# State loads asked for later, token sums moved to DVE, and four later slices in a one-core decoder step

## The chip, the core and the metric

The kernel runs on one core of a Trainium2 chip. A core has TensorE (PE, matmuls), VectorE (DVE), ScalarE (ACT), GpSimd (POOL) and SyncE (SP), which here issues the loads. The metric is the device time of one execution in microseconds; lower is better. Times are medians of runs; the profile is of one execution.

## The reference

One step of a hybrid decoder layer: 512 prompt tokens and 8 x 4 sample tokens (544 columns in all) go through one input projection of width 2048 to 8192, eight heads of stick-breaking attention and eight heads of the HGRN2 recurrence, a gated per-head norm and an output projection. All in 32-bit floats.

```
h = rmsnorm(x, norm_w);  p = h @ w_in            # q_a k_a v_a z_a | q_b f_b i_b z_b
o_a = stick_breaking(q_a, k_a, v_a)              # prompt: causal blocks; samples: 16 cached pages each
...
S_new = S * exp(bl) + (kc * exp(bl - b)).T @ vc  # per head, state 128 x 128; samples start from state_s
o_b = (qc * exp(b)) @ S + tril(qc @ kc * decay) @ vc
...
x = x + concat(norm(o_a) * silu(z_a), norm(o_b) * silu(z_b)) @ w_out;  y = rmsnorm(x, final_norm_w)
```

Outputs are the two results, the new keys and values, and the new states of the prompt and of the eight samples.

## The kernel before

Every large product is made of fp32r parts: an operand is split into a rounded half (ACT, `L304`) and a remainder (DVE, `L305`), and three products are added. A projection of 128 columns (`project`) has 24 slices of STEP = 4 units of matmuls; its two accumulators are emptied by DVE (`L454`, `L456`), and the next projection needs the same two banks.

The program runs in five stages. First the tokens are transposed and split. Then four query heads are projected plainly (`first_part`, up to 107 us), and beside them `token_sums` makes four sums of token blocks in hi and lo halves. With these, eleven pairs of column blocks are projected by a scheme of Strassen's kind with seven products for eight (`project_two`, to 340 us); their results go to DRAM. In the attention stage (to 785 us) keys and values of head h are projected, and beside them runs `attend` for the head before. In the HGRN2 stage (to 1317 us) the forget gate and input of head h are projected, and beside them `hgrn` of the head before: four score rounds (first the pairs, `finish_pairs`, then the three of ROUNDS), the update of the states (`up`, `usp`) and the outputs. The output projection ends the program.

Beside both stages runs `decode`, the attention of the samples to their cached pages, in 36 steps: a step loads two units of key pages (SP, `L687`, three buffers), DVE transposes them (`L697`), PE multiplies them (`dzp`, `L825`), and four steps later the values (`av`, `L835`) use pages from ten buffers (`L708`).

The order on PE and SP is the order in which the program is written (a manual schedule), and that is set by `Flow`: the projection's slices are the base, and after each slice up to two side slices are taken whose wait is over. A side generator yields (cost, wait, hold of a bank, share of the base that must be done); the wait is in a modelled time that adds up slice costs. So a number such as 4000.0 at `finish_head` says how many modelled nanoseconds must pass before the slice is put into PE's order. It sets the order alone: in the run every instruction waits for its operands, and what stands behind it on its engine waits too. DVE, ACT and POOL are ordered by the program's scheduler.

`finish_head` squares a head's output (POOL `L565`, `L569`; ACT `L568`), sums the squares on PE (`sp`, `L572`, `L573`) and stores the head. `hgrn` asks at its start for the head's sample states (`L875`, two tiles `bst`, two buffers in all); they are used at `osp` (`L1023`) and updated at `usp` (`L1052`, `L1055`) and stored from there by POOL (`L1057`). So the request of head h waits on SP until both stores of head h-1 are done.

Of the kernel before, what the change touches and what calls it, by code (L numbers as in the profile page):

```python
# [18 lines left out]
P = 128  # L19
# [11 lines left out]
H = 8  # L31
# [111 lines left out]
def hybrid_step(ctx: ExitStack, tc: tile.TileContext, x_prompt, x_sample, cache_k, cache_v, state_s, page_table,  # L143
# [316 lines left out]

    def token_sums(c):

# [9 lines left out]
        def less(eng, a, b):  # L472
            d, e = temp(), temp()
            eng.tensor_tensor(d, a[0], b[0], ALU.subtract)
            eng.tensor_tensor(e, a[1], b[1], ALU.subtract)
            eng.tensor_tensor(d, d, e, ALU.add)
            return d
# [11 lines left out]

        t1 = less(nc.vector, block(0, 1), block(0, 0))  # L490
        keep_sum(nc.vector, 0, t1)
        t2 = less_sum(nc.vector, block(1, 1), t1)
        keep_sum(nc.vector, 1, t2)
        keep_sum(nc.gpsimd, 3, less_sum(nc.gpsimd, block(1, 0), t2))
        keep_sum(nc.gpsimd, 2, less(nc.gpsimd, block(1, 1), block(0, 1)))

# [105 lines left out]
    def attend(h, qt, kt, vt):  # L602
# [56 lines left out]
        a_past[h] = True  # L659
        yield from finish_head(ap, h, ot, zt, 4000.0)  # L660

# [130 lines left out]
    def decode(start, stop):  # L792
# [4 lines left out]
        for step in range(NSTEP):  # L797
# [14 lines left out]
            while values and weights_ready[b - 1] is None:  # L812
                yield 0.0, 500.0, 0.0, 0.0
            yield (32 * 56.0 if keys else 0.0) + (8 * 213.0 if values else 0.0), \
                (8000.0 if step == 0 else 3000.0), 0.0, start + (stop - start) * step / NSTEP
            if keys:
# [38 lines left out]
    def hgrn(h, F, it, res):  # L855
# [15 lines left out]
        nc.gpsimd.tensor_tensor(prod[0], f2[:, :, 0], f2[:, :, 1], ALU.mult)  # L871
        sts = []
        for hf in range(2):
            st = bp_.tile([P, 4, P], F32, name="bst", bufs=2)
            nc.sync.dma_start(st, state_s[0, 4 * hf:4 * hf + 4, h].rearrange("b k v -> k b v"))  # L875
            sts.append(st)

# [37 lines left out]

        yield from scores(1, lambda n: e0[:, n * 192:(n + 1) * 192], e0[:, 688:816], 5000.0, finish_pairs)
        e = etile()
# [7 lines left out]
        for r, hl in enumerate(ROUNDS):  # L925
# [20 lines left out]
            def finish(half, sp):  # L946
# [10 lines left out]
                if half and r == 0:  # L957
# [4 lines left out]
                    nc.vector.copy_predicated(a5, m5, s5)  # L962

            yield from scores(hl, moving, e[:, 824:952] if r == 0 else None, 3000.0, finish)
            new = etile()
# [78 lines left out]
        if finish:  # L1044
            yield from finish_head(bp_, H + h, ot, res["zt"], 4000.0)
        for hf in range(2):
# [40 lines left out]

    SUMS_AT = ((1, 4), (1, 18), (2, 8), (2, 22))
    sp_ = None
    sstack = ExitStack()  # L1090

    def first_part():
        nonlocal sp_
        for h in range(PLAIN):
# [6 lines left out]
            for i, c in enumerate(project(qtile, h * P, h == 0)):  # L1101
# [6 lines left out]
                if (h, i) in SUMS_AT:  # L1108
                    token_sums(SUMS_AT.index((h, i)))
                yield c  # L1110
# [324 lines left out]
```

## Time and profile before

| | us |
|---|---|
| runs of the kernel | 1557.32 and 1562.46, median 1559.89 |
| the profiled execution | 1562.26 |
| its span, first to last instruction | 1560.5 |
| PE busy (matmuls) | 1359.2 (87%) |
| DVE / POOL / ACT busy | 879.1 / 507.6 / 473.4 |
| mean granted clock of PE | 0.933 |

The difference of 1.8 us between the execution's time and its span lies around the first and last instruction. A row of the wait view gives the waiting engine and line, what released it, and the time. PE works its slices strictly in order, so a wait of PE delays all that follows; an idle engine that nobody waits for costs nothing.

### The profile page before, as it was taken

To read this page: it belongs to the slowest core of one execution; us is meant where nothing else is said; L and a number is where in the kernel's file an instruction comes from. 1 tells how busy PE (TensorE), PEld (TensorE's weight loads), DVE (VectorE), ACT (ScalarE), POOL (GpSimd) and SP (SyncE) were. 2 spreads that over 40 slices of the span, in tenths; PEclk is the share of its full clock that TensorE was granted. 3 is DMA by queue.
4 is the path that set the end of the run, shared out by engine and by line. 5 is a ranking of instruction groups with operands and counts; after the bars stand their busy time and mean duration, and the time that the engine had idled before them with its cause. 6 is when DMAs were issued, how large, how long until landed. Compare 5 with 4: busy or idle time off the path is not lost.

```text
span 1560.5 us, 30699 instructions
## 1 busy us (share of the span) xinstructions
PE 1359.2 (87%) x11658; PEld 1215.6 (78%) x11658; DVE 879.1 (56%) x1427; ACT 473.4 (30%) x783; POOL 507.6 (33%) x723
## 2 busy tenths in 40 slices
PE   7769999998878979879878768989989889999997
PEld 6659999997766868768767557777868657889897
DVE  6866666645465554564665455576574745622223
ACT  6223343331333333333323031222222222422223
POOL 3777776650222221121222131232231222310101
PEclk9979999998988989999979879999989989999999
DMA  6224434439767967878844929898959656442223
GB/s 186 82 82 137 124 111 123 138 113 228 199 166 193 267 184 226 243 191 253 227 130 127 226 95 263 237 254 222 254 144 280 171 180 222 151 140 82 76 76 140
DMA packets 248965, 270.85 MB, mean 174 GB/s; under 512 B 14073, under 2 KB 170290, under 8 KB 248114
## 3 DMA queue, kind: packets, MB, share of 16 engines
q1 hardware_dynamic: 240048, 239.88, 55.8%
q0 software_dynamic: 6992, 21.08, 3.8%
q10 hardware_dynamic: 1778, 7.93, 1.4%
q8 instruction: 92, 1.51, 0.4%
q14 instruction: 55, 0.45, 0.1%
HBM read 244.16 MB, written 24.67 MB: 172 GB/s over the span
## 4 chain that ended last, share of the span: by engine, by line
PE 39%; issue 9%; DVE 8%; DMA 8%; ACT 3%; POOL 2%; SPq 1%; DVEq 0%; POOLq 0%; ACTq 0%
PE pacc L447 15%; PE yacc L1272 10%; PE av L835 4%; DVE kpage L697 3%; DMA kpage<-in_cache_k 3%; PE dzp L825 3%; PE sp L897 2%; DMA wraw<-in_w_in 1%; PE ysp L1281 1%; DMA ys<-in_x_sample 1%; PE usp L1052 1%; DVE wlo L305 1%; DMA m_dram<-sq 1%; PE op L655 1%; POOL sqlo L569 1%
## 5 line engine op out<-in xcount | busy, mean ns | idle before, releaser
L447 PE MATMUL pacc<-h_hi,whi 128*128 128x288 f32 (+1 forms) x1344 | 384.0, 314 | 40.2 <-DVE sq L456 25.3
L447 PE MATMUL pacc<-h_lo,whi 128*128 128x288 f32 (+1 forms) x1344 | 364.0, 298 | 0.0
L447 PEld LDWEIGHTS pacc<-h_hi,whi 128*128 128x128 f32 x1344 | 266.9, 199 | 71.7 <-issue 47.2
L447 PEld LDWEIGHTS pacc<-h_lo,whi 128*128 128x128 f32 x1344 | 267.4, 199 | 3.5 <-issue 1.7
L305 DVE TENSOR_TENSOR wlo<-wraw,whi 128x1024 fp32r<-128x1024 f32 x138 | 186.2, 1350 | 146.0 <-PE yacc L1272 70.3
L304 ACT CAST whi<-wraw 128x1024 fp32r<-128x1024 f32 x138 | 144.3, 1047 | 368.5 <-PE pacc L447 164.4
L447 PE MATMUL pacc<-h_hi,wlo 128*128 128x288 f32 (+1 forms) x1344 | 200.9, 297 | 0.0
L447 PEld LDWEIGHTS pacc<-h_hi,wlo 128*128 128x128 f32 x1344 | 181.1, 192 | 8.8 <-issue 8.0
L697 DVE STREAM_TRANSPOSE kpage<-kpage 128x2048 f32<-128x2048 f32 x64 | 146.3, 2298 | 20.2 <-DMA kpage<-in_cache_k 20.2
L825 PE MATMUL dzp<-kpage,qblk 128*32 128x128 f32 x2048 | 78.0, 306 | 67.5 <-DVE kpage L697 67.5
L1272 PE MATMUL yacc<-whi,m_hi 128*128 128x256 f32 x512 | 128.7, 290 | 0.0
L1272 PE MATMUL yacc<-whi,m_lo 128*128 128x256 f32 x512 | 124.9, 283 | 2.6 <-DVE m_lo L1262 2.6
L825 PEld LDWEIGHTS dzp<-kpage,qblk 128*32 128x32 f32 x2048 | 61.2, 123 | 79.7 <-DVE kpage L697 66.2
L1272 PEld LDWEIGHTS yacc<-whi,m_hi 128*128 128x128 f32 x512 | 97.4, 190 | 15.7 <-issue 12.4
L1272 PEld LDWEIGHTS yacc<-whi,m_lo 128*128 128x128 f32 x512 | 97.7, 191 | 3.2 <-DVE m_lo L1262 3.0
L835 PE MATMUL av<-vpage,dwt 128*32 128x512 f32 x512 | 88.1, 690 | 8.1 <-DMA vpage<-in_cache_v 8.1
L1344 POOL TENSOR_TENSOR y<-y,fnw 128x512 f32<-128x512 f32 (+1 forms) x18 | 25.2, 1419 | 179.8 <-DVE y L1340 110.5
L897 PE MATMUL sp<-bE,kr 128*128 128x192 f32 x256 | 52.0, 347 | 22.5 <-DVE kr L868 22.5
L305 DVE TENSOR_TENSOR wlo<-sraw,whi 128x1024 fp32r<-128x1024 f32 x33 | 52.4, 1589 | 28.5 <-ACT whi L304 28.5
L1272 PE MATMUL yacc<-wlo,m_hi 128*128 128x256 f32 x512 | 68.4, 282 | 0.1
L1272 PEld LDWEIGHTS yacc<-wlo,m_hi 128*128 128x128 f32 x512 | 64.3, 191 | 0.3 <-DVE wlo L305 0.3
L897 PEld LDWEIGHTS sp<-bE,kr 128*128 128x128 f32 x256 | 44.5, 203 | 24.6 <-issue 13.9
(344 smaller groups left out, 2522.7 us busy)
## 6 DMA issues: line engine op xcount, KB each, us to landing
kpage<-in_cache_k SPq DMA_DIRECT2D x256, 256.0 KB, 5.8
vpage<-in_cache_v SPq DMA_DIRECT2D x256, 256.0 KB, 5.2
wraw<-in_w_in SPq DMA_DIRECT2D x106, 512.0 KB, 6.0
wraw<-in_w_out SPq DMA_DIRECT2D x32, 512.0 KB, 3.4
sraw<-in_w_in SPq DMA_DIRECT2D x22, 512.0 KB, 5.4
p_dram<-so POOLq DMA_DIRECT2D x22, 272.0 KB, 2.9
bst<-in_state_s SPq DMA_DIRECT2D x16, 256.0 KB, 2.9
out<-bst POOLq DMA_DIRECT2D x16, 256.0 KB, 2.9
```

The costliest lines, as they stand in the source:

```text
L304: turns.append(nc.scalar.copy(hi, raw))
L305: nc.vector.tensor_tensor(lo, raw, hi.bitcast(F32), ALU.subtract)
L447: nc.tensor.matmul(ps[half][:, :n], a[:, j, :], x[:, j, ts], start=(kh == 0 and part == 0 and r == 0), stop=(kh == 1 and part == 1 and r = ...
L569: nc.gpsimd.tensor_tensor(lo, sq, hi.bitcast(F32), ALU.subtract)
L655: nc.tensor.matmul(op[:, tb * P:(tb + 1) * P], vn[:, j, :], wt[:, first[tb] + j, :], start=(j == 0), stop=(j == tb))
L697: nc.vector.transpose(flat, flat)
L825: nc.tensor.matmul(zp[32 * g:32 * g + 32, gp * P:(gp + 1) * P], qb[:, at:at + 32], kt[:, g, :, 32 * j:32 * j + 32], start=(gp == 0 and h2 ...
L835: nc.tensor.matmul(av[hf][32 * i:32 * i + 32, :], wt[:, gp, i, :], vpending[n], start=(gp == 0), stop=(gp == 3))
L897: nc.tensor.matmul(sp[:, i * 192:(i + 1) * 192], kr[:, n * P:(n + 1) * P], moving(n), start=True, stop=True)
L1052: nc.tensor.matmul(usp, kns, vb.rearrange("p b d -> p (b d)"), start=True, stop=True)
L1272: nc.tensor.matmul(out, m[4 * kq + j][:, c], b[:, j, :], start=(kq == 0 and part == 0 and r == 0 and (one or tb % 2 == 0)), stop=(kq == 3 ...
L1344: nc.gpsimd.tensor_tensor(part, part, fnw[:, cs].unsqueeze(1).to_broadcast([P, n, CG]), ALU.mult)
```

## The change

Three edits. `token_sums` is cut into two parts of four calls each, placed at eight points of the plain heads in place of four, with all its adds and subtracts on DVE; the third block sum no longer takes `t2` from the temporary but adds the halves of the second sum up again. Four waits of side slices become longer: `finish_head` of both kinds of heads 4000 to 6500, the key products of decode step 0 8000 to 18000, the first score round 5000 to 8000. The request for the sample states moves from the start of `hgrn` to the second round of ROUNDS, the third of the four score rounds.

```diff
--- before.py
+++ after.py
@@ -458,7 +458,7 @@
 
     sums = []
 
-    def token_sums(c):
+    def token_sums(part, c):
 
         j = slice(2 * c, 2 * c + 2)
         at = slice(0, XH), slice(XH, T)
@@ -487,12 +487,15 @@
             nc.scalar.copy(hi[:, j], x)
             eng.tensor_tensor(lo[:, j], x, hi[:, j].bitcast(F32), ALU.subtract)
 
-        t1 = less(nc.vector, block(0, 1), block(0, 0))
-        keep_sum(nc.vector, 0, t1)
-        t2 = less_sum(nc.vector, block(1, 1), t1)
-        keep_sum(nc.vector, 1, t2)
-        keep_sum(nc.gpsimd, 3, less_sum(nc.gpsimd, block(1, 0), t2))
-        keep_sum(nc.gpsimd, 2, less(nc.gpsimd, block(1, 1), block(0, 1)))
+        if part == 0:
+            t1 = less(nc.vector, block(0, 1), block(0, 0))
+            keep_sum(nc.vector, 0, t1)
+            keep_sum(nc.vector, 1, less_sum(nc.vector, block(1, 1), t1))
+        else:
+            keep_sum(nc.vector, 2, less(nc.vector, block(1, 1), block(0, 1)))
+            t2 = temp()
+            nc.vector.tensor_tensor(t2, sums[1][0][:, j].bitcast(F32), sums[1][1][:, j].bitcast(F32), ALU.add)
+            keep_sum(nc.vector, 3, less_sum(nc.vector, block(1, 0), t2))
 
     def project_two(pair, n, done):
         a = ps_acc.tile([P, 512], F32, name="pa", tag="acc")
@@ -657,7 +660,7 @@
         ot = ap.tile([P, SEQ], F32, name="ot", bufs=1)
         nc.vector.tensor_copy(ot, op)
         a_past[h] = True
-        yield from finish_head(ap, h, ot, zt, 4000.0)
+        yield from finish_head(ap, h, ot, zt, 6500.0)
 
 
     def page_value(held, b, gp, i):
@@ -812,7 +815,7 @@
             while values and weights_ready[b - 1] is None:
                 yield 0.0, 500.0, 0.0, 0.0
             yield (32 * 56.0 if keys else 0.0) + (8 * 213.0 if values else 0.0), \
-                (8000.0 if step == 0 else 3000.0), 0.0, start + (stop - start) * step / NSTEP
+                (18000.0 if step == 0 else 3000.0), 0.0, start + (stop - start) * step / NSTEP
             if keys:
                 if quarter == 0:
                     zp = ps_z.tile([P, 512], F32, name="dzp", tag="z")
@@ -869,11 +872,6 @@
         prod = [bp_.tile([P, n], F32, name=f"prod{n}") for n in (T // 2, 64, 16, 4)]
         tots = bp_.tile([P, DB], F32, name="tots")
         nc.gpsimd.tensor_tensor(prod[0], f2[:, :, 0], f2[:, :, 1], ALU.mult)
-        sts = []
-        for hf in range(2):
-            st = bp_.tile([P, 4, P], F32, name="bst", bufs=2)
-            nc.sync.dma_start(st, state_s[0, 4 * hf:4 * hf + 4, h].rearrange("b k v -> k b v"))
-            sts.append(st)
 
         yield 5 * TR, 900.0, 1500.0, 0.0
         tp = gbank("vtp")
@@ -913,7 +911,7 @@
                 nc.vector.tensor_tensor(a3, s3[:, :, 0:2], eye[:NS, :NS // 2], ALU.mult)
                 nc.vector.copy_predicated(a3[:, :, 1], sub[:NS, :NS // 2], s3[:, :, 2])
 
-        yield from scores(1, lambda n: e0[:, n * 192:(n + 1) * 192], e0[:, 688:816], 5000.0, finish_pairs)
+        yield from scores(1, lambda n: e0[:, n * 192:(n + 1) * 192], e0[:, 688:816], 8000.0, finish_pairs)
         e = etile()
         nat = e.rearrange("p (u y) -> p u y", y=14)[:, :, :8].rearrange("p u (j i) -> p u j i", i=2)
         ev = e3[:, :, 0:3:2].rearrange("p (u j) x -> p u j x", j=4)
@@ -961,6 +959,12 @@
                     s5 = sp[:NS, 456:].rearrange("p (u s i) -> p u s i", s=7, i=2)[:, :, 1:4:2]
                     nc.vector.copy_predicated(a5, m5, s5)
 
+            if r == 1:
+                sts = []
+                for hf in range(2):
+                    st = bp_.tile([P, 4, P], F32, name="bst", bufs=2)
+                    nc.sync.dma_start(st, state_s[0, 4 * hf:4 * hf + 4, h].rearrange("b k v -> k b v"))
+                    sts.append(st)
             yield from scores(hl, moving, e[:, 824:952] if r == 0 else None, 3000.0, finish)
             new = etile()
             grp = 4 if r < len(ROUNDS) - 1 else 1
@@ -1042,7 +1046,7 @@
         nc.vector.tensor_reduce(o_s[:, H + h, :], tp[:, :P].rearrange("p (j t) -> p t j", j=4), axis=AX.X, op=ALU.add)
         hg_past[h] = True
         if finish:
-            yield from finish_head(bp_, H + h, ot, res["zt"], 4000.0)
+            yield from finish_head(bp_, H + h, ot, res["zt"], 6500.0)
         for hf in range(2):
             vb = bp_.tile([P, NB, P], F32, name="bkn")[:NS]
             nc.gpsimd.tensor_tensor(vb, vs.unsqueeze(1).to_broadcast([NS, 4, P]),
@@ -1085,7 +1089,7 @@
         if col < W:
             nc.gpsimd.tensor_copy(q_new[:, col // P, :], out[:, SEQ:])
 
-    SUMS_AT = ((1, 4), (1, 18), (2, 8), (2, 22))
+    SUMS_AT = ((1, 2), (1, 10), (1, 18), (2, 2), (2, 10), (2, 18), (3, 4), (3, 12))
     sp_ = None
     sstack = ExitStack()
 
@@ -1106,7 +1110,7 @@
                     for n in range(4):
                         sums.append([sp_.tile([P, NK // 2, XH], F32R, name=f"sum{n}{m}") for m in ("hi", "lo")])
                 if (h, i) in SUMS_AT:
-                    token_sums(SUMS_AT.index((h, i)))
+                    token_sums(*divmod(SUMS_AT.index((h, i)), 4))
                 yield c
             store_part(h * P, qts[0])
         for n, pair in enumerate(couples):
```

The order on PE, counted in slices of the projections (four matmuls each) that stand ahead:

| slice | before | changed |
|---|---|---|
| key products of decode step 0, 1, 31 | 576, 610, 1403 | 598, 628, 1422 |
| last four value steps (32 to 35) | 1423, 1427, 1434, 1438 | 1442, 1446, 1446, 1446 |
| last slice ahead of the final gate's projection | 1446 | 1446 |
| sum of squares, attention heads 0 to 7 | 660, 706, 752, 798, 851, 895, 941, 990 | 662, 709, 758, 803, 849, 903, 947, 990 |
| first scores, HGRN2 heads 0, 1, 2 | 1000, 1051, 1092 | 1010, 1058, 1106 |
| sum of squares, HGRN2 heads 0, 1 | 1041, 1089 | 1050, 1104 |
| second state update of HGRN2 heads 0, 1 | 1055, 1096 | 1060, 1113 |

On DVE, in the third plain head's stretch; `so` are temporaries, `sum0lo` to `sum3lo` the low halves of the sums, `sq<-pacc` evictions, `wlo` a weight piece's remainder. Before:

```order
L305 TENSOR_TENSOR wlo<-wraw,whi 128x1024
L488 TENSOR_TENSOR sum1lo<-so,sum1hi 128x544
L474 TENSOR_TENSOR so<-h_hi_98 128x544
L475 TENSOR_TENSOR so<-h_lo_99 128x544
L476 TENSOR_TENSOR so<-so 128x544
L481 TENSOR_TENSOR so<-h_hi_100,so 128x544
L482 TENSOR_TENSOR so<-so,h_lo_101 128x544
L456 TENSOR_TENSOR sq<-pacc,rbc 128x256
```

In the changed kernel:

```order
L305 TENSOR_TENSOR wlo<-wraw,whi 128x1024
L488 TENSOR_TENSOR sum2lo<-so,sum2hi 128x544
L482 TENSOR_TENSOR so<-so,h_lo_101 128x544
L474 TENSOR_TENSOR so<-h_hi_100,h_hi_98 128x544
L475 TENSOR_TENSOR so<-h_lo_101,h_lo_99 128x544
L488 TENSOR_TENSOR sum3lo<-so,sum3hi 128x544
L476 TENSOR_TENSOR so<-so 128x544
L497 TENSOR_TENSOR so<-sum1hi,sum1lo 128x544
L456 TENSOR_TENSOR sq<-pacc,rbc 128x256
```

The third and fourth sums (`sum2lo`, `sum3lo`), which stood on POOL, now stand on DVE between the evictions, with the new add at `L497`.

On SP, around the state request of HGRN2 head 1 (`kr` a head's queries, `zt` its gate, `kpage` and `vpage` cached keys and values, `wraw` weights). Before:

```order
L708 DMA vpage<-in_cache_v 128x512
L559 DMA zt<-p_dram 128x544
L853 DMA kr<-p_dram 128x544
L257 DMA wraw<-in_w_in 128x8x128
L875 DMA bst<-in_state_s 128x4x128 x2
L257 DMA wraw<-in_w_in 128x8x128
L687 ISA
L687 DMA kpage<-in_cache_k 32x4x512
```

In the changed kernel:

```order
L711 DMA vpage<-in_cache_v 128x512
L966 DMA bst<-in_state_s 128x4x128 x2
L257 DMA wraw<-in_w_in 128x8x128 x2
L562 DMA zt<-p_dram 128x544
L856 DMA kr<-p_dram 128x544
L690 ISA
L690 DMA kpage<-in_cache_k 32x4x512
```

The request now stands behind the sixteen page loads of a decode step and ahead of two weight pieces, the head's own gate and head 2's queries; before, it stood right behind head 1's queries and a weight piece, ahead of a step's page loads.

## Rows read from the trace of the kernel before

**Rows 1.** Busy time by window, three stages: us and instructions, granted clock.
```profile
40.06:107.41 67.35, 40.72 (x291) 39.65 (x290) 49.35 (x46) 16.04 (x22) 54.46 (x36) 0.82 0.29 82
...
340.00:785.00 445.00, 372.48 (x3452) 331.47 (x3450) 247.38 (x371) 143.31 (x258) 99.84 (x201) 0.90 0.79 217
785.00:1317.50 532.50, 450.94 (x3944) 376.57 (x3943) 321.34 (x702) 122.89 (x192) 141.34 (x316) 0.91 0.73 203
```

**Rows 2.** Waits of PE, 40 to 108 us: total us, times, longest.
```profile
PE pacc L447 <- DVE sq L456: 25.3, 3, 16.8
```

**Rows 3.** The same view, PE, 340 to 785 us.
```profile
PE dzp L825 <- DVE kpage L697: 38.1, 9, 6.9
PE sp L573 <- POOL sqlo L569: 12.9, 5, 3.9
PE kvsp L176 <- DVE z L611: 4.9, 4, 3.5
...
PE vnp L176 <- DVE z L611: 2.8, 1, 2.8
```

**Rows 4.** The same view, PE, 785 to 1317.5 us.
```profile
PE dzp L825 <- DVE kpage L697: 29.5, 10, 9.3
PE sp L897 <- DVE kr L868: 22.5, 3, 10.6
PE sp L573 <- POOL sqlo L569: 9.0, 2, 7.3
PE av L835 <- DMA vpage<-in_cache_v: 8.1, 2, 7.5
```

**Rows 5.** The same view, SP's queue, 785 to 1317.5 us.
```profile
SPq L875 <- DMA out<-bst: 128.1, 12, 27.6
```

**Rows 6.** DVE by line, 40 to 108 us: busy us, mean ns, idle before.
```profile
L305 DVE TENSOR_TENSOR wlo<-wraw,whi 128x1024 fp32r<-128x1024 f32 x6 | 11.3, 1880 | 8.7 <-ACT whi L304 8.0 <-ACT sum1hi L487 0.7
...
L476 DVE TENSOR_TENSOR so<-so 128x544 f32<-128x544 f32 x4 | 4.9, 1230 | 0.1
...
L456 DVE TENSOR_TENSOR sq<-pacc,rbc 128x256 f32<-128x256 f32 x8 | 3.3, 415 | 0.1
L482 DVE TENSOR_TENSOR so<-so,h_lo 128x544 f32<-128x544 f32 x4 | 2.9, 722 | 0.1
L305 DVE TENSOR_TENSOR wlo<-ssum,whi 128x1024 fp32r<-128x1024 f32 x1 | 1.2, 1209 | 0.0
```

**Rows 7.** DVE by line, 43 to 46 us, where POOL stands.
```profile
L481 DVE TENSOR_TENSOR so<-h_hi,so 128x544 f32<-128x544 f32 x1 | 0.7, 725 | 0.0
```

**Rows 8.** Timeline, PE, decode step 0: start, us, idle before.
```profile
354.77 1.94 PE L825 MATMUL dzp<-kpage,qblk 128*32 128x128 f32 x32 [6.35 <-DVE kpage L697]
359.23 1.08 PE L825 MATMUL dzp<-kpage,qblk 128*32 128x128 f32 x16 [2.52 <-DVE kpage L697]
```

**Rows 9.** Busy time by window after a wait of PE; clock before DMA share.
```profile
92.00:95.00 3.00, 3.00 (x15) 3.00 (x15) 3.00 (x3) 0.00 (x0) 3.00 (x3) 0.50 0.00 0
96.00:99.00 3.00, 3.00 (x26) 3.00 (x25) 1.36 (x1) 0.65 (x1) 3.00 (x4) 1.00 0.06 15
```

**Rows 10.** Timeline, ACT, 364 to 366 us.
```profile
364.60 1.05 ACT L304 CAST whi<-wraw 128x1024 fp32r<-128x1024 f32 x1 [20.05 <-DMA wraw<-in_w_in]
```

**Rows 11.** Timeline, DVE, 378 to 385 us.
```profile
378.68 4.50 DVE L697 STREAM_TRANSPOSE kpage<-kpage 128x2048 f32<-128x2048 f32 x2
```

**Rows 12.** Timeline, SP, 852 to 864 us: HGRN2 head 1's states.
```profile
852.03 11.77 SPq L875 DMA_DIRECT2D bst<-in_state_s  x2
```

**Rows 13.** Timeline, PE, waits for key pages near 877 and 1165 us.
```profile
877.35 1.06 PE L825 MATMUL dzp<-kpage,qblk 128*32 128x128 f32 x13 [9.28 <-DVE kpage L697]
...
1164.96 1.30 PE L825 MATMUL dzp<-kpage,qblk 128*32 128x128 f32 x20 [3.35 <-DVE kpage L697]
```

**Rows 14.** The instructions of line 825: min/median/max ns, first and last start.
```profile
L825 PE MATMUL dzp<-kpage,qblk x2048: 272/273/424, 354.8 to 1245.2; 128*32 128x128 f32 x187
```

**Rows 15.** Timeline, SP, 1246 to 1254 us: eight value pages.
```profile
1247.00 6.20 SPq L708 DMA_DIRECT2D vpage<-in_cache_v  x8
```

## The prediction

> **What bounds the kernel now.** I read the busy times by stage first [rows 1]. From 40 to 107 us, the columns computed without Strassen's scheme, TensorE (PE) is busy 40.72 of 67.35 us, with DVE at 49.35 and POOL at 54.46. In the attention stage (340 to 785) PE is busy 372.48 of 445 us, in the HGRN2 stage (785 to 1317.5) 450.94 of 532.5. What can be won is PE's idle time: 27 us, then 73, then 82. The lists of who waited for whom name the causes. In the first stretch PE waits 25.3 us in three waits for the copies out of PSUM on DVE [rows 2]. In the attention stage the largest wait is for transposed key pages, 38.1 us in nine, then 12.9 us in five for the low half of the squares that POOL makes [rows 3]. In the HGRN2 stage it is key pages again (29.5 us in ten), then `kr` at a head's first score products (22.5 us in three, the longest 10.6), the squares (9.0) and value pages (8.1) [rows 4]. SP, the queue of all loads, stands 128.1 us in that stage at line 875, where a head asks for its sample states while their buffers are still being stored by the head before [rows 5].
>
> **Token sums.** PE's accumulators are emptied by DVE, which is slow while POOL works beside it: a weight piece's remainder takes 1880 ns on average and 1209 after POOL's share is done; of the sum ops, L476 takes 1230 ns, and L482, which mostly meets no POOL op, 722 [rows 6]. Between 43 and 46 us, with POOL idle, a sum op takes 725 ns [rows 7]. The change leaves POOL nothing of this and gives DVE 60 ops in place of 28 (the second sum is added up again from its halves, four ops more than the two engines had). In the changed order 57 of them stand before the eviction with which the Strassen part may start, with six weight remainders and nine evictions. At the lengths without POOL: 57 x 0.72 = 41.0, 6 x 1.21 = 7.3, and 9 evictions of at most 0.415 are 3.7, together 52.0 us from 40.06: the Strassen part starts at 92.1, now at 107.41: **-15.3**. DVE stays the bound there; PE's own three columns would be done earlier. If ops follow each other faster than they last, it is up to -20; if they stay at today's middle, 1230 ns, and a piece at 1880, DVE needs 57 x 1.23 + 6 x 1.88 + 3.7 = 85.1 us, and the part starts at 125.2, 17.8 later.
>
> That last case has an advocate. The Trainium skill (Perfetto Trace Analysis, section Optimizing Scalar/DVE Operations) says that where DVE is saturated, offloading work to GpSimd may make sense, though the two share a read port. This change goes the other way and loads DVE, on which PE waits; by the offloading rule alone it would lose those 17.8 us, by the port it gains. Rows 6 and 7 speak for the port.
>
> **Decode step 0.** Its key products move from slice 576 to slice 598. PE now waits there 6.35 and 2.52 us, from 348.4 on [rows 8]. A slice of four matmuls takes 0.46 us at full clock (26 in 3.00 us [rows 9]), so 22 slices are 10.1 us: PE comes at 358.5, just as the second unit is turned (359.2). But what PE does in their place needs a weight piece four slices earlier, at 356.7, whose copy on ACT starts only at 364.60, when its load has landed among the key pages [rows 10]. In the changed order this load goes ahead of eight page loads; I let it land up to 5 us earlier, which leaves a wait of 4 to 9 us. From -5 to 0, taken as **-3**. Further, two transposes of 4.50 us [rows 11] no longer stand on DVE ahead of the first head's logits, for which PE waits 2.8 us and up to 3.5 [rows 3]: **-4.5**.
>
> **Finishing the heads.** The slice of the squares comes 2.5 us of the planner's time later, some five slices where nothing else intervenes. Counted from the products before it, its distance grows in five attention heads and shrinks in two: of 12.9 us [rows 3] I take **-8**. In the HGRN2 stage the wait of 7.3 us gets six slices more (2.8 us), and at the other one a decode step no longer lies between: of 9.0 [rows 4], **-4**.
>
> **First scores.** They stand 10, 7 and 14 slices later in heads 0, 1 and 2, that is 4.6, 3.2 and 6.4 us; in head 2 a decode step is gone from in front, which takes part of that back. Of 22.5 us [rows 4]: 5, 3.2 and 4, **-12.2**.
>
> **State request.** At head 1 the states' two loads are issued at 852.03 and, 11.77 us later, done [rows 12]; key pages queue behind, and PE waits 9.28 us for them at 877 [rows 13]. The same at head 5: 3.35 us at 1165 [rows 13]. In the changed order the request stands after the second score round. At head 1 it comes behind 16 page loads, when both stores of the head before are long done; at heads 3 to 7 the update products of the head before stand ten slices or more ahead. At head 2 alone the second update comes two slices after the request, and I count nothing there. The states' own load is hidden by the third and fourth score rounds, over ten slices; without them it would cost PE one landing. **-12.7**. At head 7 the value pages' wait of up to 7.5 us [rows 4] goes too, but decode now stands 19 slices later: the last three value steps come where no projection slice is left, and wait for their pages; I count 0.
>
> **Clock.** After a long wait PE runs at half its clock: granted 0.50 (1.2 GHz) from 92 to 95 us, 15 matmuls in 3 us after a wait of 16.8 [rows 2], and 1.00 (2.4 GHz) from 96 to 99, with 26 [rows 9]. Such a stretch costs 3.0 x 11/26 = 1.3 us; three waits of over 5 us go: **-4**.
>
> **The sum.** The attention stage gives 3 + 4.5 + 8 = 15.5, the HGRN2 stage 12.2 + 4 + 12.7 = 28.9, the clock 4: 48.4. Not all of it stays. PE works in order, and a wait removed brings it earlier to the next decode step, where it often waits for key pages anyway: 19 such waits in the two stages [rows 3, 4], two of them at step 0 and two behind a state request, so 15 of 32 steps have one that nothing here touches, some of them short. I take 0.4 of the 48.4 as given back, 19.4, and 29 as kept. With the sums: -44.3. The profiled execution took 1562.3 us (span 1560.5 and 1.8 around it), 2.4 above the median of 1559.9. On the median: 1559.9 - 44.3 = **1515.6**.
>
> **Rivals.**
> - *Nothing is given back* (0.17): all of 63.7 us, 1496. For it: 17 of 32 steps have no wait for pages. Against it: the other 15.
> - *Waits only move* (0.20): of the two stages only the 4.5 us of the first logits stay, 1559.9 - 19.8 = 1540. For it: every decode step shifts by about 20 slices against the heads, which deals the waits anew.
> - *The state request still blocks* (0.08): asked later, it only meets a later store. Then 0.6 x 14 = 8.4 us are missing: 1524. The order at head 2 speaks for it, that at the others against.
> - *Decode becomes what ends last* (0.05): page load, transposes, keys, values set the end of the HGRN2 stage, and waits removed elsewhere are worth nothing. Its steps are 28.7 us apart (354.8 to 1245.2 in 31 steps [rows 14]). It starts 10.1 us later, with some 6 for the weight piece in front, and its last three value steps, whose eight loads hold SP 6.2 us each [rows 15], 19 in all, lie beside no slices: 1559.9 - 15.3 + 10 + 6 + 19 = 1580. It decides if the spacing stays at 28.5 or more; the forecast needs 27.9.
> - *DVE's ops stay long without POOL* (0.04), the offloading case above: 33 us more than the forecast, 1549.
>
> The forecast itself has 0.46, with 1497 to 1534 as its own range.
>
> **How the numbers follow.** A measurement of this kernel can tell about 2% from no change, here 1529 to 1591. Of the forecast's 0.46 some 0.43 lies below 1529; with the first rival and most of the third that makes 0.68 for faster. The second, the fifth and the rest make 0.28 for within 2%, and the fourth most of the 0.04 for slower. The range of 1484 to 1545 takes in the first three rivals and leaves out the last two and the far ends.
>
> **What would show it.** Right: sum ops of about 0.72 us, the Strassen part starting near 92 us, no state request that holds SP over 5 us except at head 2, first scores waiting about 10 us in all, decode steps about 27.9 us apart. Wrong: sum ops over 1 us with POOL idle; waits for key pages that grow by what the others lose; PE idle for 20 us or more around the last value steps.

## The result, and the profile after

The changed kernel takes 1503.26 us (median of 2 runs, 1500.52 and 1506.01) against 1559.89: a ratio of 0.964, interval 0.954 to 0.974, so 56.6 us less where 44.3 were forecast. The time lies inside the range. The profiled execution took 1500.52 us, span 1498.8. The sum came out near the time, but not its parts, and that is what the runs below are about.

Busy time by window of the changed kernel (us, then busy us and instructions of PE, its weight loads, DVE, ACT and POOL, granted clock, DMA share, GB/s). The first window runs from the first sum to the eviction that lets the Strassen part start. The last one takes in the attention and the HGRN2 stage; the two between part it at 785 us, where the kernel before goes from the one to the other. The changed kernel does so some 40 us earlier (the first scores of HGRN2 head 0 start at 754.73, before at 795.90), so its row from 785 us on leaves out the start of its HGRN2 stage:

```profile
43.66:93.65 49.99, 39.72 (x284) 38.69 (x284) 49.82 (x72) 15.03 (x20) 8.46 (x8) 0.90 0.40 111
310.00:785.00 475.00, 406.55 (x3855) 364.55 (x3858) 283.82 (x446) 159.53 (x288) 120.37 (x238) 0.94 0.79 213
785.00:1272.30 487.30, 430.48 (x3809) 359.84 (x3801) 301.31 (x658) 118.24 (x181) 137.12 (x291) 0.93 0.77 215
310.00:1272.30 962.30, 837.03 (x7656) 724.40 (x7655) 585.13 (x1104) 277.77 (x468) 257.48 (x529) 0.94 0.78 214
```

DVE is now the one engine that is full in the first window (49.82 of 49.99 us), and POOL has almost left it [rows 1]. For the two stages together the measure used below runs from the last start of a Strassen product with `sum0` (a few us before that part ends) to the first output product, both read from the lists of instructions. The same stretch of the kernel before is this row:

```profile
323.00:1335.70 1012.70, 858.63 (x7656) 740.37 (x7654) 586.04 (x1104) 279.63 (x468) 254.52 (x529) 0.91 0.74 203
```

So the stages became 50.4 us shorter, that point of the Strassen part comes 13.0 us earlier (323.0 to 310.0), and the output stage took 1.7 us more: 61.7 of span. Of the 50.4, PE's idle time gives 28.8 (154.1 to 125.3) and PE's busy time 21.6 (858.6 to 837.0), for the same 7,656 matmuls. The latter is put down to the clock, whose granted mean rose from 0.91 to 0.94: PE ran a smaller part of the matmuls at its lower level.

What PE waits for in the changed kernel, over the whole span (us in total, times, longest):

```profile
PE dzp L828 <- DVE kpage L700: 40.7, 12, 8.2
PE sp L895 <- DVE kr L871: 26.5, 3, 13.8
PE pacc L447 <- ACT whi L304: 11.0, 3, 8.8
PE pacc L447 <- DVE sq L456: 10.3, 4, 5.2
PE sp L895 <- issue: 6.6, 1, 6.6
PE sp L576 <- POOL sqlo L572: 6.3, 3, 4.5
...
PE av L838 <- DMA vpage<-in_cache_v: 1.9, 3, 0.9
```

Against [rows 2 to 4]: key pages fell from 67.6 to 40.7, squares from 21.9 to 6.3, value pages from 8.1 to 1.9. The first scores (`kr`) rose from 22.5 to 33.1 us: 26.5, and the 6.6 of the line `issue`, which is head 0's (its `kr` was done at 754.49, 0.24 us before the scores start). By head, the wait fell at head 0 (10.6 to 6.6) and rose at head 1 (5.7 to 10.4) and head 2 (6.2 to 13.9); 2.3 us are new at head 7. SP's queue and the first sums answer to [rows 5] and [rows 6]; the first line below is from the list of SP's waits, the others from DVE by line, 40 to 95 us (count, then busy us and mean ns):

```profile
SPq L966 <- DMA out<-bst: 43.3, 4, 24.5
```

Of the 43.3 us, 37.0 stand at head 2 and 6.3 at head 7. In the lines that follow, the mean of L481 is raised by one op beside POOL, which is shown further below.

```profile
L481 DVE TENSOR_TENSOR so<-h_hi,so 128x544 f32<-128x544 f32 x8 | 7.9, 993 | 0.1
L476 DVE TENSOR_TENSOR so<-so 128x544 f32<-128x544 f32 x8 | 5.8, 724 | 0.1
L482 DVE TENSOR_TENSOR so<-so,h_lo 128x544 f32<-128x544 f32 x8 | 5.8, 721 | 0.0
```

### The profile page after: what moved, and what is told of

Its sections match the earlier page's. It is cut to its first block, busy times and chain, and to the rows that moved or that the text cites. A ratio compares the mean times of both kernels' runs of the same rounds, so it can differ in the third digit from the quotient of the medians.

```text
span 1498.8 us, 30690 instructions
## 1 busy us (share of the span) xinstructions
PE 1342.8 (90%) x11658; PEld 1204.6 (80%) x11658; DVE 882.5 (59%) x1459; ACT 471.9 (31%) x783; POOL 465.2 (31%) x695
## 4 chain that ended last, share of the span: by engine, by line
PE 37%; DMA 5%; DVE 4%; issue 2%; ACT 1%; POOL 1%; SPq 0%; POOLq 0%; DVEq 0%; ACTq 0%
PE yacc L1276 12%; PE pacc L447 12%; PE av L838 2%; PE sp L895 2%; PE dzp L828 2%; DVE kpage L700 2%; DMA wraw<-in_w_in 2%; DMA vpage<-in_cache_v 1%; PE ysp L1285 1%; DMA kpage<-in_cache_k 1%; DMA m_dram<-sq 1%; PE usp L1056 1%; PE op L1036 0%; DVE wlo L305 0%; PE up L1010 0%
## 5 line engine op out<-in xcount | busy, mean ns | idle before, releaser
L447 PE MATMUL pacc<-h_hi,whi 128*128 128x288 f32 (+1 forms) x1344 | 376.3, 310 | 27.1 <-ACT whi L304 11.0
L447 PE MATMUL pacc<-h_lo,whi 128*128 128x288 f32 (+1 forms) x1344 | 357.4, 295 | 0.0
L447 PEld LDWEIGHTS pacc<-h_hi,whi 128*128 128x128 f32 x1344 | 262.4, 195 | 54.7 <-issue 29.0
L447 PEld LDWEIGHTS pacc<-h_lo,whi 128*128 128x128 f32 x1344 | 262.8, 196 | 2.9 <-issue 1.7
L447 PE MATMUL pacc<-h_hi,wlo 128*128 128x288 f32 (+1 forms) x1344 | 204.6, 299 | 0.0
L447 PEld LDWEIGHTS pacc<-h_hi,wlo 128*128 128x128 f32 x1344 | 182.7, 194 | 13.6 <-issue 12.3
L1276 PE MATMUL yacc<-whi,m_hi 128*128 128x256 f32 x512 | 130.8, 294 | 0.0
L828 PE MATMUL dzp<-kpage,qblk 128*32 128x128 f32 x2048 | 71.2, 290 | 40.7 <-DVE kpage L700 40.7
L828 PEld LDWEIGHTS dzp<-kpage,qblk 128*32 128x32 f32 x2048 | 57.0, 116 | 52.4 <-DVE kpage L700 44.5
L895 PE MATMUL sp<-bE,kr 128*128 128x192 f32 x256 | 52.8, 350 | 34.4 <-DVE kr L871 26.5
L838 PE MATMUL av<-vpage,dwt 128*32 128x512 f32 x512 | 79.5, 681 | 1.9 <-DMA vpage<-in_cache_v 1.9
L895 PEld LDWEIGHTS sp<-bE,kr 128*128 128x128 f32 x256 | 44.3, 203 | 38.2 <-issue 35.3
```

What stands on the lines that cost most here:

```text
L447: nc.tensor.matmul(ps[half][:, :n], a[:, j, :], x[:, j, ts], start=(kh == 0 and part == 0 and r == 0), stop=(kh == 1 and part == 1 and r = ...
L828: nc.tensor.matmul(zp[32 * g:32 * g + 32, gp * P:(gp + 1) * P], qb[:, at:at + 32], kt[:, g, :, 32 * j:32 * j + 32], start=(gp == 0 and h2 ...
L838: nc.tensor.matmul(av[hf][32 * i:32 * i + 32, :], wt[:, gp, i, :], vpending[n], start=(gp == 0), stop=(gp == 3))
L895: nc.tensor.matmul(sp[:, i * 192:(i + 1) * 192], kr[:, n * P:(n + 1) * P], moving(n), start=True, stop=True)
L1276: nc.tensor.matmul(out, m[4 * kq + j][:, c], b[:, j, :], start=(kq == 0 and part == 0 and r == 0 and (one or tb % 2 == 0)), stop=(kq == 3 ...
```

## The experiments

All runs are given as a ratio to the kernel before, timed beside it on the same chip, with its 95% interval; "us" behind a ratio is the ratio's distance from 1 times 1559.9.

### Each part alone

`sums_alone`: the kernel before with the new `token_sums`, its call and its eight places.

> The kernel before with the token sums alone as in the change (two goes, all on DVE, eight places). Own theory: DVE's sum ops last 0.72 us without POOL beside them, the Strassen part starts some 15 us earlier, and all of it stays, since PE is busy without a gap from there to the attention stage: 15.3 us less, about 1545. First rival: it is DVE's number of ops that counts (60 in place of 28), and POOL's share was a help: 10 to 18 us more, about 1570 to 1578. Second rival: the gain is given back in the attention stage, since page loads start no earlier: within 5 us of the kernel before.

`sums_dve_one_go`: the same with the old places, both goes at once (lines of `sums_alone` against this run):

```
-    SUMS_AT = ((1, 2), (1, 10), (1, 18), (2, 2), (2, 10), (2, 18), (3, 4), (3, 12))
+    SUMS_AT = ((1, 4), (1, 18), (2, 8), (2, 22))
...
-                    token_sums(*divmod(SUMS_AT.index((h, i)), 4))
+                    part = SUMS_AT.index((h, i))
+                    token_sums(0, part)
+                    token_sums(1, part)
```

> The kernel before with all sums of a token block on DVE, but in one go of 15 ops at the four places that the kernel before has. If only the read port that POOL shares with DVE counts, this gains as much as the two goes do, about 15 us (1545). If the spreading counts, since PE's evictions stand in DVE's queue behind 15 ops (15 x 0.72 = 10.8 us) in place of 7 or 8, PE waits longer at each of the four places and it gains 5 us or less.

`state_alone`: the kernel before with the two loads of the sample states moved from the start of `hgrn` to `if r == 1`.

> The kernel before with the state request alone moved to the third score round. Own theory: key-page waits of 9.3 and 3.4 us behind the request go, 12.7 us less, of which 0.6 stays: 7.6 to 12.7 less, 1547 to 1552. Rival: the pages that arrive earlier only let PE wait at the next step for something else, 0 to 3 us less. Other rival: the request matters for all later pages too, since SP stood 128 us at it in all, and the key-page waits of the whole HGRN2 stage (29.5 us) fall by half or more: 15 to 25 us less.

`later_alone`: the kernel before with the four longer waits (6500, 6500, 18000, 8000).

> The kernel before with the four longer planner waits alone (finishing of heads in both stages, decode step 0, first scores). As forecast: step 0 3, first logits 4.5, finishing 8 and 4, first scores 12.2, together 31.7, of which 0.6 stays: 19 us less, about 1541. By the trace of the changed kernel: step 0 gives nothing, first scores nothing, squares 15, and what is left of the 57 us after the sums (15) and the state request (up to 13) would be 25 to 30, so a part of the fallen key-page waits (27 us) belongs to the moved slices: 1530 to 1535. If the waits only move: 0 to 5 us less.

Measured: sums alone 0.990 (0.986 to 0.994), 15.6 us less; in one go 0.993 (0.991 to 0.996), 10.3 less; state request alone 0.976 (0.971 to 0.980), 38 us less, above all three expectations (25 at most); later slices alone 0.978 (0.974 to 0.982), 34 less, near the reading of the changed kernel's trace (1530 to 1535) and not near the forecast's terms (1541). PE's waits for DVE in the sums' stretch, first with two goes, then with one go:

```profile
PE pacc L447 <- DVE sq L456: 10.3, 4, 5.1
```

```profile
PE pacc L447 <- DVE sq L456: 17.5, 3, 11.6
```

Both versions gain, so leaving POOL out is what counts first. It can act in two ways, and no run separates them: ops beside POOL are longer, and DVE and POOL take turns at the four buffers of the temporaries `so`. A line of the kernel before, DVE from 40 to 108 us, shows the second one:

```profile
L475 DVE TENSOR_TENSOR so<-h_lo 128x544 f32<-128x544 f32 x4 | 6.3, 1564 | 8.5 <-POOL so L476 5.3 <-POOL sum3lo L488 3.2
```

Before, DVE was idle for 18.0 of the 67.35 us [rows 1], 8.5 of them waiting for POOL to be done with a temporary and 8.7 for the rounded half of a weight piece [rows 6]; in the changed kernel it is idle for 0.2 us. Its busy time is the same (49.35 and 49.82 us, 46 and 72 instructions): the shorter ops pay for the added ones, and what is won is the idle time. The longest wait of PE falls from 11.6 to 5.1 us when the sums come in two goes, as the rival of the spreading has it, and that would be the other 5 us (the intervals overlap, so neither its size nor that it is there is settled). The offloading rival, which wanted 10 to 18 us more, falls. That the two engines stand in each other's way is seen inside the changed kernel, where POOL has two sums of weight pieces left. POOL's timeline, then DVE's, around the same microseconds (start, us); POOL had been idle for 14.43 us before the first op:

```profile
75.71 2.37 POOL L288 TENSOR_TENSOR ssum<-sraw,wraw 128x1024 f32<-128x1024 f32 x1 [14.43 <-DMA wraw<-in_w_in]
78.16 2.71 POOL L290 TENSOR_TENSOR sraw<-wraw,sraw 128x1024 f32<-128x1024 f32 x1
```

```profile
73.64 0.72 DVE L488 TENSOR_TENSOR sum3lo<-so,sum3hi 128x544 fp32r<-128x544 f32 x1
...
75.87 2.79 DVE L488 TENSOR_TENSOR sum2lo<-so,sum2hi 128x544 fp32r<-128x544 f32 x1
78.58 2.87 DVE L481 TENSOR_TENSOR so<-h_hi,so 128x544 f32<-128x544 f32 x1
```

The same op of line 488 takes 2.79 us beside POOL and 0.72 while POOL is idle. Each of the two long DVE ops ends 0.6 us after the POOL op that had started before it (75.71 + 2.37 = 78.08, and 75.87 + 2.79 = 78.66). The Trainium skill (SBUF — State Buffer, section Who interferes with whom) says that a DVE instruction with two SBUF inputs contends with a GpSimd one that reads SBUF, and calls the ports that the two share an exclusive lock; these rows agree.

The state request was worth three times its term. PE's waits of `state_alone` in the HGRN2 stage:

```profile
PE sp L892 <- DVE kr L868: 24.2, 3, 10.6
PE dzp L825 <- DVE kpage L697: 11.6, 9, 2.1
PE sp L573 <- POOL sqlo L569: 9.0, 2, 7.3
PE detp L176 <- DVE bst L1056: 5.0, 1, 5.0
```

Key pages fell from 29.5 us [rows 4] to 11.6: the 9.28 and 3.35 of the forecast are gone [rows 13], and with them 5.55 us at head 2, where nothing had been counted. The value pages' 7.5 us are gone too, while squares and `kr` stay, and 5.0 us for `bst` are new. Over both stages PE's idle time falls by 22.7 us, and its busy time by 13.7 (858.6 to 844.9).

### The parts beside each other

15.6, 38 and 34 us make 88, but all of them together gave 57; 88 lies outside its interval (41 to 73). Two runs take one part out of the change.

`sums_later`: the change without the moved state request.

> The changed kernel without its state request (token sums and the four later slices). Alone, the state request took 36 us off and the later slices 34; the whole change took 57 with 15 for the sums. Theory: both edits take away the same waits (key pages at heads 1 and 2, value pages at the end), so beside the later slices the state request is worth only 5 to 12 us: about 1563 - 15 - 34 = 1513. If the edits added up and only the sums lost their gain beside them, this run would be at about 1529.

`sums_state`: the change without the four longer waits.

> The changed kernel without its four later slices (token sums and the state request). By the theory that the state request and the later slices take away the same waits: 1563 - 15 - 36 = about 1512, and the later slices are worth 5 to 12 us on top. Rival: the sums lose their gain where the state request is moved too (the attention stage starts earlier and waits for the same loads): about 1526.

Measured: 0.972 (0.967 to 0.976), 44.5 us less, and 0.968 (0.964 to 0.971), 50.7 less. Within the intervals the sums add up with either of the others (15.6 + 34 = 50, 15.6 + 38 = 54); the rivals of both runs (1529 and 1526) fall. The state request and the later slices overlap: behind the other one, the first is worth about 12 us and the second about 6 by the medians, not 38 and 34. The change's wide interval leaves these two sizes open. The idle time of the two stages says where: 154.1 before, 131.4 with the request moved, 131.0 with later slices, 125.3 with both, so 17.0 us of waits are counted twice. That is a little over half of the 31 us that do not add up; PE's busy time does not add up either (13.7, 11.0 and, for the sums, 7.9 us less alone, 21.6 together). Key pages fell by 17.5 and 20.1 us alone and by 26.8 together (10.8 twice), value pages by 7.8 and 5.9 alone and by 6.2 together (7.5 twice). Either edit alone already frees PE of the waits behind SP's blocked queue: one by not blocking it, the other by moving the decode steps some 20 slices away from the point where it blocks (in `later_alone` SP stands as long at line 875 as before, 135.5 us).

Three more runs take one of the four waits out.

`no_fin_b` (`finish_head(bp_, ..., 4000.0)`):

> The changed kernel with the finishing of the HGRN2 heads back at 4000. Theory: the later finishing slice makes the store of a finished head later, the sigmoid of the next head waits for that store (6.1 and 6.6 us on ACT, for one of two shared buffers), and so kr is late for the first scores at heads 1 and 2 (10.4 and 13.9 us on PE). Back at 4000 the two waits for kr fall to 5 to 8 us each, while the waits for the squares come back at 2 to 7 us each: within 5 us of the changed kernel (1503). Rival: the store is beside the point, kr stays as late, and the squares' waits come on top: 5 to 9 us more.

`no_scores` (`scores(1, ..., 5000.0, finish_pairs)`):

> The changed kernel with a head's first scores back at 5000. By the forecast's term of 12.2 us for the later first scores, with 0.6 of it kept, the time rises by 4 to 12 us, to 1507 to 1515, and the waits for kr grow. Theory: kr comes a fixed 13 to 18 us after the finishing product of the head before, whatever stands in between (13.1 and 14.9 us in the kernel before, 14.8 and 15.3 in the changed one), so the first scores' own due time counts for nothing where the finishing product moves with them: in this order 5.7 us of PE work stand between the two at heads 1 and 2, in place of 3.9 and 1.1, PE waits 8 to 11 us at each, and the time is 0 to 6 us less: 1497 to 1503.

`no_step0` (`8000.0 if step == 0`):

> The changed kernel with decode step 0 back at 8000. Trace reading: step 0's wait for key pages (8.9 us in the kernel before) went, and a wait of 8.8 us for a weight piece stands at the same place in the changed one, so the later step 0 gave nothing by itself: within 4 us of 1503, and the wait for pages is back at step 0. The forecast gave it 3 us and 4.5 for the first logits, with 0.6 kept: 1506 to 1511. If it is the later decode that saved the pages and values at the end (value pages 8.1 to 1.9 us), 10 us or more are lost: above 1513.

Measured: 0.960 (0.956 to 0.964), 0.970 (0.966 to 0.973) and 0.969 (0.964 to 0.972), beside 0.964 of the change. Against the change's own wide interval none of them is settled alone. By the medians `no_fin_b` is 5 us faster than the change, `no_scores` and `no_step0` 9 and 8 slower, though all four waits together are worth only 6. The two slower ones lie outside what their trace readings gave (1497 to 1503, and within 4 us), and about where the forecast's own terms put them (1507 to 1515 and 1506 to 1511; measured 1512.3 and 1511.5). In `no_scores`, though, the time does not come back at the first scores, whose waits fall from 33.1 to 31.1. So a due time has no price of its own here; it has one beside the others. PE's waits of `no_scores` from 784 us on:

```profile
PE sp L895 <- DVE kr L871: 21.0, 3, 8.0
PE dzp L828 <- DVE kpage L700: 14.1, 11, 3.6
PE sp L576 <- POOL sqlo L572: 9.5, 2, 4.7
PE pacc L447 <- DVE bi L456: 5.3, 1, 5.3
```

`kr` behaves as its theory says at heads 1 and 2 (8.0 and 7.5 us, single waits of the timeline, in place of 10.4 and 13.9), while head 0's wait rises from 6.6 to 10.1; and the squares' wait is back with 9.5 us, although their slice still has 6500. In `no_fin_b` the squares of the HGRN2 heads do not wait at all, although theirs is back at 4000, and `kr` waits 9.8 and 14.0 us at heads 1 and 2, where 5 to 8 had been expected: its time came out within the 5 us, but not by its theory. Which slices stand between two others is thus set by all four numbers together. In `no_step0` the wait for pages is back at step 0 (6.63 and 2.52 us), and the first head's two waits for `z` are back too (2.55 and 3.26), and key pages rise from 40.7 to 57.4 us over both stages. Of the 57.4, 9.2 are step 0's, in whose place the weight piece's 8.8 us stand in the change, so the later start of decode was worth nothing at step 0 and 7.5 us of key pages behind it. The squares rise by 5.5, and the first scores fall by 7.6 (33.1 to 25.5, head 0 included).

### What held the first scores

In the changed kernel the chain of work that ended last goes through two stores of a finished head (start, us):

```profile
802.06 4.20 DMA m_dram<-sq
...
864.52 4.70 DMA m_dram<-sq
```

ACT's timeline around the first one, then PE's first scores of heads 1 and 2:

```profile
798.90 0.69 ACT L215 ACTIVATE sq<-sp,eps 128x512 f32<-128x512 f32 x1 [1.43 <-PE sp L576]
799.62 0.63 ACT L216 ACTIVATE sq<-sq 128x512 f32<-128x512 f32 x1
806.33 0.66 ACT L219 ACTIVATE sgm<-kr 128x544 f32<-128x544 f32 x1 [6.08 <-DMA m_dram<-sq]
```

```profile
813.26 0.98 PE L895 MATMUL sp<-bE,kr 128*128 128x192 f32 x2 [10.41 <-DVE kr L871]
...
876.22 1.30 PE L895 MATMUL sp<-bE,kr 128*128 128x192 f32 x3 [13.85 <-DVE kr L871]
```

`sq` of a head that is being finished and `sgm` of the next head share two buffers (tag `sg`). The finished head's squares, root and product all live in `sq`, so the buffer is free only when the store has landed, and the sigmoid, the first op on the way to `kr`, waits for it. From the finishing product (line 573 before, 576 after) to the first scores it takes 13.1 and 14.9 us at heads 1 and 2 in the kernel before, 14.8 and 15.3 in the changed one, and 16.9 and 18.4 in `no_fin_b`. There, at head 2, a page transpose of 2.30 us stands on DVE between the two products of the finishing (L579 and L586), and the sigmoid waits 9.64 us for the store; so an earlier finishing product did not make `kr` earlier by as much. PE waits for what this chain lasts beyond the work that stands in between. The test frees the buffer early and leaves nothing out.

`sq_early`, the change with, in `finish_head`, for the HGRN2 heads:

```
-        rs = sq
-        rsqrt_mean(rs, sp, P)
-        nc.vector.scalar_tensor_tensor(rs, ot, gains[:, hh:hh + 1], rs, ALU.mult, ALU.mult)
+        if hh >= H:
+            rsqrt_mean(sp, sp, P)
+            rs = ot
+            nc.vector.scalar_tensor_tensor(rs, ot, gains[:, hh:hh + 1], sp, ALU.mult, ALU.mult)
+        else:
...
```

(The `else` branch holds the three old lines.)

> The changed kernel, where in the HGRN2 stage the finishing of a head no longer holds the shared buffer until its store: the reciprocal root is made in PSUM and the product in the head's own output tile, so the buffer is free after the low half of the squares. Nothing is left out. Theory of the store and the shared buffer: ACT's waits of 6.1 and 6.6 us for the store go, kr is ready that much earlier, PE's waits for it (10.4 and 13.9 us) fall to some 4 and 7, and the kernel gains 5 to 12 us: 1491 to 1498. Rival: kr is late because the head's first slices come too close behind the query's load or behind other work on DVE; then the waits for kr stay above 20 us in all and the time stays within 3 us of 1503.

Measured: 0.939 (0.935 to 0.944), 95 us less than before and 38 less than the change, three times the upper end of what was expected. ACT's sigmoid at the same place, and PE's waits from 785 us on:

```profile
789.16 0.66 ACT L219 ACTIVATE sgm<-kr 128x544 f32<-128x544 f32 x1 [0.98 <-POOL sqlo L572]
```

```profile
PE dzp L833 <- DVE kpage L705: 15.2, 7, 3.1
PE detp L176 <- DVE bst L1064: 3.7, 1, 3.7
PE sp L900 <- DVE kr L876: 3.3, 2, 2.3
```

The sigmoid now starts before the finishing product, not 7.5 us after it, and the waits of 24.3 us at heads 1 and 2 shrink to 1.0 for `kr` and 2.6 for a later op of DVE (`bot`, L580). I had counted only the landing of the store as won, while the whole way through product, root and store went. The stages need 927.5 us in place of 962.3: 31.0 less idle, some 21 of them at these scores, and 3.8 less busy. Where the other 10 of idle time came from was not followed.

`before_sq_early`, the same edit on the kernel before:

> The kernel before with the one edit that gave 38 us on the changed kernel: the finishing of an HGRN2 head frees the shared buffer after the low half of the squares. Theory: the waits for kr at heads 1 and 2 (5.7 and 6.2 us) go, the one at head 0 (10.6 us, no head before it) stays; on the changed kernel 24.3 us of such waits were worth 35 in the two stages, so 11.9 us are worth about 17: 1541 to 1549. If the changed kernel's gain came from elsewhere (its first scores had become worse by the change), 0 to 5 us here: above 1554.

Measured: 0.992 (0.989 to 0.996), 12 us less (7 to 18), where 17 were expected. `kr` waits only at head 0, but another copy of DVE's queue comes late instead:

```profile
PE sp L902 <- DVE kr L873: 10.9, 1, 10.9
PE sp L902 <- DVE bvs L893: 10.1, 2, 6.6
```

DVE's timeline at head 1:

```profile
846.52 0.28 DVE L893 COPY bvs<-vstp 32x128 f32<-32x128 f32 x1 [2.32 <-POOL bkn L1053]
```

PE's second pair of first scores waits for the copy `bvs`, and that one for POOL, which makes the state updates of the head before from the same tile. So the shared buffer is shown to be the cause of `kr`'s waits at heads 1 and 2 in both kernels. In the kernel before it is one of two causes that end close together: `kr` and `bvs` make 21.0 us where `kr` alone made 22.5. The idle time of the two stages falls by 7.6 us there, 4.5 of it at key pages, so most of the 12 us is not won at the first scores themselves.

`sq_early_fin_b`, `sq_early` with `no_fin_b`:

> The kernel with the early buffer (1465), and the finishing of the HGRN2 heads back at 4000. Theory: with the buffer free early nothing hangs on the finishing product, so its place is free again; without the state request in front the squares did not wait in the HGRN2 stage at 4000 either: within 4 us of 1465. If the later place was what kept PE from waiting for the squares, 7 to 9 us come back at one or two heads: 1472 to 1478.

Measured: 0.935 (0.931 to 0.938), 102 us less than before, the fastest version here: 1458.5 us beside 1465.1, with intervals that overlap. The 7 to 9 us of the other expectation did not come back.

## Why the prediction was right or wrong

- **Token sums, -15.3: right.** Alone 15.6. From the first sum to the eviction it takes 50.0 us where 52.0 were worked out, with ops of 0.72 us; the Strassen part starts at 93.65 where 92.1 was forecast, in an execution that reaches the first sum 3.6 us later. The forecast gave the length of the ops as the only reason; that DVE was idle for 18.0 us of the stretch, 8.5 of them for POOL's temporaries, it did not say.
- **State request, -12.7: right in its mechanism, a third of its size.** Alone 38 us, of which the two stages show 22.7 of idle and 13.7 of busy time. The step that failed is to count only the two waits whose cause could be read at the request (12.6 us), nothing at head 2 (5.55 us) and 0 for the value pages (7.5), and to price the clock for three waits only. Beside the later slices it is about 12, near the term, but by another way: those had already taken the rest.
- **First scores, -12.2: wrong.** The waits rose from 22.5 to 33.1 us. At head 0 the term was near: 4.1 less, where 5 were counted. At heads 1 and 2 the step that failed is this: "They stand 10, 7 and 14 slices later" was counted against the projection, but `kr` hangs on the finishing product of the head before, and edit and edit moved both. Between the two, the wait itself left out, 7.4 and 8.7 us passed on PE before and 4.4 and 1.4 after. The forecast never followed `kr` back past DVE.
- **Finishing heads, -12: the squares' waits fell by 15.6,** but not by their own due time in the HGRN2 stage (`no_fin_b`), and the 9.0 us that were won there stand against 12.3 more at the first scores of heads 1 and 2.
- **Step 0, -3: 0 at its place.** The upper bound held: a wait of 8.79 us for the weight piece stands at 353.29, where 6.35 and 2.52 for pages went [rows 8]. What the later decode brings behind it (7.5 us of key pages) had no term.
- **First logits, -4.5: right.** PE's two waits for `z` at the first head, 2.76 and 3.50 us, are gone, and `no_step0` brings them back. At the next head new waits of 2.39 and 1.25 stand in the changed kernel, so 2.6 to 6.3 us were won.
- **Given back, +19.4: wrong in sign for key pages,** which fell by 26.8 us. Key pages, squares and value pages together fell by 48.6, and the idle time of the two stages by 28.8, so part did come back, but at other waits, 10.6 of it at the first scores. That the 28.8 lie near the forecast's 26.6 (0.6 of the 44.4 without the clock) is chance, made of a term that failed and others that were too small.
- **Clock, -4: too small.** The matmuls of the two stages were busy 21.6 us less, of which some 8 can be one execution's (last section). In windows of 2 us, counted over both stages, the clock was below 0.75 in 26 stretches, 180 us of windows, before, and in 19, 126 us, after. I priced only three waits of over 5 us; in the changed kernel the granted clock was also 0.50 from 1098 to 1100 us, behind a wait of 3.08 us.
- **The sum.** In the profiled executions 61.7 us were won, 17.4 more than forecast: idle time 28.8 in place of 26.6, busy time 21.6 in place of 2.4 (0.6 of 4), the Strassen part 13.0 earlier in place of 15.3, and 1.7 more in the output stage. So what the forecast was short of is PE's busy time.
- **Rivals.** By its time alone (1496) "nothing is given back" is nearer to 1503 than the forecast's 1515.6, but it falls by the waits: some came back. Decode does not end last: its steps are 27.2 us apart (356.9 to 1199.0), under 28.5. "Waits only move" holds for the first scores of heads 1 and 2 alone. DVE's ops did not stay long (0.72 us). The state request still blocks, 37.0 of 43.3 us at head 2, as forecast. Two signs of being right did not come: first scores waiting about 10 us in all (33.1), and, narrowly, no other request that holds SP over 5 us (6.0 at head 7).

What stays open is why `no_scores` and `no_step0` cost 9 and 8 us while all four waits together bring 6, if the medians are right: the traces show which waits come back, not a rule for it.

## What to carry to other kernels

A slice that waits is as late as the event it hangs on: follow the wait back through every engine, buffers and stores included, and count the distance from that event; moving the slice and the event together gained nothing at heads 1 and 2 here. Two edits that clear the same queue or the same waits must not be added: price each alone and each as the last one. A shared buffer that holds a value until its DMA has landed is a wait that none of the due times tried here removed. What freeing it is worth depends on what else ends close by: 38 us in the changed kernel, where the four due times bring 6, and 12 in the kernel before, where they bring 34.

## What the runs showed of the hardware

The cost of idle time was more than the idle time in these runs. The same 7,656 matmuls of the two stages were busy 858.6 us in the kernel before, 837.0 in the changed one and 822.8 in the fastest, where the granted clock of the stages is 0.91, 0.94 and 0.96 on average. Not all of it follows from the waits: `sums_alone` has the same idle time in these stages as the kernel before (153.8 and 154.1 us), and yet 7.9 us less busy time at 0.93. `sums_later` and `no_step0`, with 130.8 us of idle time each, differ by 11 us of busy time. So some 8 to 11 us of such a difference can be one execution's.
